# The down product of a feed forward as seven block products over four inner tiles, in turns with the up product

## The chip, the cores and the metric

The kernel runs on one core of one Trainium2 chip. The metric is the device time of one execution in microseconds (us), the median of several runs. A core has a matrix engine (TensorE, PE in the profile; its weight loads are PEld), three engines for elementwise work (VectorE or DVE, ScalarE or ACT, GpSimd or POOL) and a queue that issues transfers (SyncE, SP). SBUF is the on-chip memory, PSUM holds the sums of the matrix engine in eight banks, and HBM is the large memory outside.

## The reference

One layer of an encoder trunk for 2048 prompt tokens and 32 sample tokens, 1024 channels, all in float32. After a mixer (spatial gating and a gated delta rule, which the change does not touch) comes a feed forward with 4096 inner channels:

```python
h = rmsnorm(x, norm_ffn_g[l]) * (1 + sc2) + sh2
x = x + gt2 * (jnp.square(jax.nn.relu(h @ w_up[l])) @ w_down[l])
...
y = rmsnorm(x, final_norm_g)
```

`w_up` is 1024 x 4096 and `w_down` 4096 x 1024.

## The kernel before, in words

**Precision.** Every float32 operand of a matmul is kept as two parts in a reduced format: `hi` is a rounded copy (one ACT operation), `lo` the rest (one DVE subtraction, `split`). A product is three matmuls, hi·hi, hi·lo and lo·hi, into one PSUM bank (`mm3`); one matmul here is 128 x 128 weights against 260 token columns.

**Stages.** The mixer ends near 1047 us of the span; from there to the end runs the feed forward. Activations lie with channels on the partitions and tokens in the columns. The 2080 tokens are cut into four blocks `b` of 520, each of two column groups `g` of 260. The 4096 inner channels are cut into 16 pairs `s` of two 128-channel tiles `m`. For each block and each `s` the kernel computes the up product of that pair (`ffn_up`), squares its positive part, and adds its share to the down product (`ffn_down`, one step later), whose sums `acc` stay in SBUF for all 1024 outputs (eight tiles `m` by two groups `g`).

**Up product.** It is already done in a seven-product block form (in place of eight): the inputs of a block are combined once into seven sets of four tiles `hp[0..6]`, which go through HBM as `th_d` (`h2_values`, `h2_load`), and the weights of a pair are seven tiles of 128 x 512: three plain quadrants and four sums. In block 0 the sums are formed on POOL and stored to HBM (`su_d`); in later blocks they are read back as float32 and split again. Seven products of 12 matmuls are 84 matmuls for a pair.

**Down product.** Plain: for each `s`, each `g` and each of the eight outputs `m`, two inner tiles by three matmuls, 6 matmuls in a bank, then one DVE operation (`stt`, line 1574) which multiplies the bank by the gate and adds it to `acc`. For a pair that makes 96 matmuls and 16 DVE operations. The weights of a pair are two tiles of 128 x 1024, loaded and split (`down_weights`). The up product has four PSUM banks, the down product three. A hidden tile is relu and square on ACT, its square again on POOL in full precision, and the rest of it on DVE.

**End of a block.** The last pair squares the sums and adds them up, forms the norm of a token from them, scales, and writes `yT` (`final`); meanwhile the inputs of the next block are split into `hp`.

**Order.** The program is first recorded as operations with their regions of memory; a planner (`schedule`) then lays them out on the engines by readiness, by a class of urgency and, within the matmul classes, by the place of the matmul that they feed. It works with a table of costs that is written in the kernel, so the order on each engine is fixed before the run. All transfers are issued by SP, in one order, each waiting until its buffer is free. Buffers are taken in turn from rings.

## Time and profile before

| what | value |
|---|---|
| median of 3 runs | 2475.16 us (2473.93 to 2476.86) |
| profiled execution | 2478.63 us, span 2476.8 us |
| feed forward in it | 1047 to 2476.8 us |
| PE busy, of the span | 2422.7 us (98%) |
| DVE, ACT, POOL busy | 1870.6, 1256.6, 734.9 us |
| bytes moved | 461.00 MB, mean 186 GB/s |
| granted TensorE clock | 0.996 |

Busy time is the union of an engine's instructions. A matmul is shown with about 0.28 us, but they are pipelined, and one starts every 0.12 us; the same holds in a smaller measure on DVE and ACT, where an instruction starts before the one ahead has ended. So what an engine can do is read from the distance of starts, not from the durations. In the tables by stage the columns are the length of the stage, the busy time of each engine with its number of instructions, the granted clock (PEclk), the busy share of the 16 DMA engines and what they moved.

### The profile page before, as it was taken

To read this page: it belongs to the slowest core of one execution; us is meant where nothing else is said; L and a number is where in the kernel's file an instruction comes from. 1 tells how busy PE (TensorE), PEld (TensorE's weight loads), DVE (VectorE), ACT (ScalarE), POOL (GpSimd) and SP (SyncE) were. 2 spreads that over 40 slices of the span, in tenths; PEclk is the share of its full clock that TensorE was granted. 3 is DMA by queue.
4 is the path that set the end of the run, shared out by engine and by line. 5 is a ranking of instruction groups with operands and counts; after the bars stand their busy time and mean duration, and the time that the engine had idled before them with its cause. 6 is when DMAs were issued, how large, how long until landed. Compare 5 with 4: busy or idle time off the path is not lost.

```text
span 2476.8 us, 53101 instructions
## 1 busy us (share of the span) xinstructions
PE 2422.7 (98%) x19338; PEld 2271.0 (92%) x19338; DVE 1870.6 (76%) x4180; ACT 1256.6 (51%) x2840; POOL 734.9 (30%) x1072
## 2 busy tenths in 40 slices
PE   7999999999999999999999999999999999999998
PEld 3877788999989779999999999999999999999998
DVE  5556666556655555589988999888998888888887
ACT  4555556465565434454444654444754445644443
POOL 2134423212422223364443442111621111611112
PEclk9999999999999999999999999999999999999999
DMA  8688667455457767766554576444675444744431
GB/s 302 212 292 280 190 220 241 146 177 166 139 177 218 245 209 244 239 213 192 181 168 157 168 229 212 141 137 131 202 229 184 137 132 150 219 138 137 130 117 45
DMA packets 308750, 461.00 MB, mean 186 GB/s; under 512 B 62636, under 2 KB 192576, under 8 KB 308488
## 3 DMA queue, kind: packets, MB, share of 16 engines
q1 hardware_dynamic: 308488, 457.61, 58.7%
q8 instruction: 152, 2.49, 0.4%
q14 instruction: 110, 0.90, 0.1%
HBM read 354.59 MB, written 102.90 MB: 185 GB/s over the span
## 4 chain that ended last, share of the span: by engine, by line
PE 76%; DMA 8%; DVE 6%; ACT 3%; issue 3%; POOL 2%; SPq 1%; DVEq 0%; POOLq 0%; ACTq 0%
PE g L397 47%; PE u L397 21%; PE C L397 3%; DVE s L356 2%; POOL s L351 2%; PE B L397 2%; ACT s L336 2%; DVE s L351 2%; DVE wl L351 1%; PE L L397 1%; SPq L389 1%; PE M L397 1%; DMA s<-th_d 1%; ACT wh L336 1%; PE L L408 1%
## 5 line engine op out<-in xcount | busy, mean ns | idle before, releaser
L336 ACT ACTIVATE s<-s 128x260 f32<-128x260 f32 (+9 forms) x807 | 383.4, 481 | 615.1 <-PE g L397 430.9
L351 POOL TENSOR_TENSOR s<-s 128x260 f32<-128x260 f32 (+17 forms) x569 | 358.9, 634 | 897.4 <-ACT s L336 781.9
L356 DVE SCALAR_TENSOR_TENSOR s<-g,modc,s 128x260 f32<-128x260 f32 (+5 forms) x1200 | 526.1, 459 | 124.2 <-PE g L397 100.1
L397 PE MATMUL g<-s,s 128*128 128x260 f32 x4032 | 502.6, 284 | 5.9 <-DVE s L356 5.3
L397 PE MATMUL u<-BH,wh 128*128 128x260 f32 x1792 | 508.2, 284 | 0.0
L397 PE MATMUL u<-BL,wh 128*128 128x260 f32 x1792 | 506.4, 283 | 0.0
L397 PE MATMUL u<-BH,wl 128*128 128x260 f32 x1792 | 505.9, 282 | 0.4 <-DVE wl L351 0.4
L397 PEld LDWEIGHTS g<-s,s 128*128 128x128 f32 x4032 | 491.7, 188 | 10.4 <-DVE s L356 9.0
L397 PE MATMUL g<-BH,wh 128*128 128x512 f32 (+3 forms) x1144 | 431.7, 377 | 0.7 <-DVE s L356 0.7
L397 PE MATMUL g<-BH,wl 128*128 128x512 f32 (+3 forms) x1144 | 401.7, 351 | 0.0
L397 PE MATMUL g<-BL,wh 128*128 128x512 f32 (+3 forms) x1144 | 400.5, 350 | 0.8 <-DVE BL L351 0.8
L351 DVE TENSOR_TENSOR wl<-s,wh 128x512 fp32r<-128x512 f32 (+1 forms) x453 | 347.8, 781 | 28.2 <-ACT wh L336 24.1
L336 ACT ACTIVATE wh<-s 128x512 fp32r<-128x512 f32 (+1 forms) x453 | 284.8, 632 | 109.8 <-PE u L397 92.4
L397 PEld LDWEIGHTS u<-BH,wl 128*128 128x128 f32 x1792 | 337.2, 188 | 0.6 <-DVE wl L351 0.6
L397 PEld LDWEIGHTS u<-BH,wh 128*128 128x128 f32 x1792 | 337.5, 188 | 0.2
L397 PEld LDWEIGHTS u<-BL,wh 128*128 128x128 f32 x1792 | 337.5, 188 | 0.0
L351 POOL TENSOR_TENSOR s<-s,s 128x260 f32<-128x260 f32 (+3 forms) x195 | 222.4, 1150 | 296.2 <-ACT s L336 151.2
L351 DVE TENSOR_TENSOR s<-s,s 128x260 fp32r<-128x260 f32 (+7 forms) x400 | 237.7, 598 | 60.9 <-POOL s L351 30.8
L397 PE MATMUL g<-BH,s 128*128 128x260 f32 x1344 | 253.2, 285 | 4.3 <-DVE s L356 3.8
L397 PEld LDWEIGHTS g<-BH,wh 128*128 128x128 f32 x1144 | 217.1, 190 | 27.3 <-issue 9.1
L397 PEld LDWEIGHTS g<-BH,wl 128*128 128x128 f32 x1144 | 216.0, 189 | 19.4
L397 PEld LDWEIGHTS g<-BL,wh 128*128 128x128 f32 x1144 | 217.2, 190 | 15.4 <-DVE BL L351 1.5
(102 smaller groups left out, 3300.1 us busy)
## 6 DMA issues: line engine op xcount, KB each, us to landing
s<-w_u SPq DMA_DIRECT2D x208, 256.0 KB, 3.3
s<-su_d SPq DMA_DIRECT2D x192, 256.0 KB, 4.1
s<-w_d SPq DMA_DIRECT2D x64, 512.0 KB, 4.0
wr<-w_d SPq DMA_DIRECT2D x64, 512.0 KB, 5.2
wr<-w_b SPq DMA_DIRECT2D x42, 512.0 KB, 4.8
s<-x_d SPq DMA_DIRECT2D x128, 130.0 KB, 3.1
s<-adaw SPq DMA_DIRECT2D x32, 512.0 KB, 5.0
s<-kq_d SPq DMA_DIRECT2D x64, 256.0 KB, 3.3
```

What stands on the lines that cost most here:

```text
L336: self.p.op(ACT, c, lambda: nc.scalar.activation(out=R(out), in_=R(in_), func=func, **{k: R(v) for k, v in kw.items()}), [out, accum], [in ...
L351: self.p.op(eng, c, lambda: e.tensor_tensor(out=R(out), in0=R(a), in1=R(b), op=op), [out], [a, b])
L356: self.p.op(DVE, c, lambda: nc.vector.scalar_tensor_tensor(out=R(out), in0=R(a), scalar=R(s), in1=R(b), op0=op0, op1=op1), [out], [a, s, b])
L389: self.p.op(DMA, max(500, x), lambda: nc.sync.dma_start(out=R(out), in_=R(in_)), [out], [in_], lat=DMA_LATENCY + min(0, x - 500))
L397: nc.tensor.matmul(R(out), R(l), R(r), **kw)
L408: self.p.op(PE, 114, lambda: nc.tensor.transpose(R(out), R(in_), R(ident)), [out], [in_, ident])
```

## The change

**Down product.** Two pairs `s`, so four inner tiles, are taken together as `q` (eight per block). The four hidden blocks are B11 and B12 (first pair, groups 0 and 1) and B21, B22 (second pair). From them come T1 = B12 - B11, T2 = B22 - T1, T3 = B22 - B12 and T4 = B21 - T2 (`hidden`, on POOL), and each of the seven operands is split. The weights are combined the same way: three plain quadrants and four sums S1 to S4. Each half `u` of the outputs then takes seven products of 12 matmuls (`ffn_down`). A bank of the first set, B1, is filled by B11 and read, then T2 is added in the same bank and it is read again, and so on with T1 and B22: four reads of a bank that is never cleared between. Block 0, and the last `q` of the last block, stay plain with all four inner tiles in one bank (`ffn_down8`).

**Turns.** The up product of a pair is recorded behind each half `u` of the down product. All eight banks are one pool (`take`, `give`).

**Stored parts.** The four up sums of the weights are stored in block 0 as both parts, hi and lo (`su_d[s][i][e]`), and read back as two tiles with an ACT copy each, where one tile was read and split before. The sums of the down weights are stored in `sd_d`: for even `u` in block 0, for odd `u` in block 1.

**The rest.** The sums stay without gate until q = 6, when `settle` multiplies them by the gate and adds the residual; from then on `add` works with the gate. Every second lo part of the next block's inputs is formed on POOL. Half of the final scalings go from POOL and ACT to DVE. A hidden tile's lo part is taken from the ACT square.

```diff
-        self.su_d = [[dt(f"su_d{s}_{i}", [P, 512]) for i in range(4)] for s in range(16)]
+        self.su_d = [[[dt(f"su_d{s}_{i}{e}", [P, 512]) for e in range(2)] for i in range(4)] for s in range(16)]
+        self.sd_d = [[dt(f"sd_d{u}_{i}", [P, 512]) for i in range(4)] for u in range(16)]
...
-                self.split(*self.hp[i][k], x)
+                self.split(*self.hp[i][k], x, POOL if b and k % 2 else DVE)
...
+        def sum_(i, x):
+            if b == 0:
+                hl = self.operand(self.uw, x)
+                for e in range(2):
+                    self.dma(self.su_d[s][i][e], hl[e].f32())
+            else:
+                hl = self.turn(self.uw)
+                for e in range(2):
+                    self.act(hl[e], self.raw(self.uraw, self.su_d[s][i][e]), AF.Copy)
+            out.append(hl)
...
+        else:
+            for x in (quad(0), sd[2], sd[1], quad(1), sd[0], quad(3), sd[3]):
+                yield self.operand(self.dw, get(x))
+
+    def plain(self, b, q):
+        return b == 0 or (b, q) == (NB - 1, 7)
...
+                for u, _ in enumerate(self.ffn_down8(b, q, ops) if self.plain(b, q) else self.ffn_down(b, q, ops)):
+                    if q < 7 and u < 2:
+                        up(b, 2 * q + 2 + u, then)
...
-                for so, sw, q in self.fsegs(b, g):
-                    ss = slice(so, so + sw)
-                    self.stt(a[:, ss], ps[:, ss], self.modc[:, 5, m, q : q + 1], x[:, ss] if s == 0 else a[:, ss], ALU.mult, ALU.add)
...
+        if q == 0 and first:
+            self.act(a, ps, AF.Copy)
+        elif q < SETTLE:
+            self.tt(a, ps, a, ALU.add)
...
+            product("T3", B2, True, w[u])
+            add(B2, hi, 1, True)
+            product("T2", B1[u], False, w[u])
+            add(B1[u], hi, 0, True)
+            B3 = [self.take() for _ in lo]
+            product("B21", B3, True, w[u])
+            add(B3, lo, 0, last=True)
+            self.give(*B3)
+            product("T1", B1[u], False, w[u])
+            add(B1[u], hi, 1, last=True)
+            product("T4", B2, False, w[u])
+            add(B2, hi, 0, last=True)
+            self.give(*B2)
+            product("B22", B1[u], False, w[u])
+            add(B1[u], lo, 1, True, True)
+            self.give(*B1[u])
+            yield
```

**How it moves the order on DVE.** In the middle of a block, the additions of the down product. `g` and `f` are PSUM banks, a number is one use of a bank, `s_289` to `s_292` (before) and `s_417` to `s_420` (now) are pieces of SBUF that hold the sums, `modc` the gate. Before:

```order
L356 SCALAR_TENSOR_TENSOR s_289<-g_23630,modc,s_289 128x260
L356 SCALAR_TENSOR_TENSOR s_289<-g_23638,modc,s_289 128x260
L356 SCALAR_TENSOR_TENSOR s_290<-g_23646,modc,s_290 128x260
L356 SCALAR_TENSOR_TENSOR s_290<-g_23654,modc,s_290 128x260
L356 SCALAR_TENSOR_TENSOR s_291<-g_23662,modc,s_291 128x260
L356 SCALAR_TENSOR_TENSOR s_291<-g_23670,modc,s_291 128x260
```

Now:

```order
L352 TENSOR_TENSOR s_418<-f_18467,s_418 128x260
L352 TENSOR_TENSOR s_418<-f_18478,s_418 128x260
L352 TENSOR_TENSOR wl<-wr_96,wh 128x512
L352 TENSOR_TENSOR s_420<-f_18483,s_420 128x260
L352 TENSOR_TENSOR s_420<-f_18487,s_420 128x260
L352 TENSOR_TENSOR s_9896<-s_426,s_10062 128x512
L352 TENSOR_TENSOR s_420<-f_18467,s_420 128x260
L352 TENSOR_TENSOR s_10863<-s_428,s_10863 128x260
L352 TENSOR_TENSOR s_420<-f_18478,s_420 128x260
```

A bank was read once and left; now the banks `f_18467` and `f_18478` are read, filled further, and read again, with splits of weights (128x512) and of hidden tiles (`s_10863`) between.

**How it moves the order on PE.** At the same place, with `f_18467` and `f_18478` the two banks of B1. Before, one output of the down product, in one bank:

```order
L397 MATMUL g_19415<-BH_78,s_925 128x260
L397 MATMUL g_19415<-BL_86,s_925 128x260
L397 MATMUL g_19415<-BH_78,s_9976 128x260
L397 MATMUL g_19415<-BH_78,s_10697 128x260
L397 MATMUL g_19415<-BL_86,s_10697 128x260
L397 MATMUL g_19415<-BH_78,s_9859 128x260
```

Now, the third product, T2, into the banks that B11 had filled 12 matmuls of T3 before:

```order
L398 MATMUL f_18487<-BH_78,s_10105 128x260
L398 MATMUL f_18467<-s_10865,s_1053 128x260
L398 MATMUL f_18467<-s_11827,s_1053 128x260
L398 MATMUL f_18467<-s_10865,s_10105 128x260
L398 MATMUL f_18467<-BH_78,s_1053 128x260
L398 MATMUL f_18467<-BL_86,s_1053 128x260
L398 MATMUL f_18467<-BH_78,s_10105 128x260
L398 MATMUL f_18478<-s_10865,s_1053 128x260
```

An output takes as many matmuls in one visit to a bank as before, but the bank has to have been read before the visit begins.

**How it moves the order on SP.** In the middle of a block, reads of weights. Before:

```order
L389 DMA s_277<-su_d_1_214 128x512
L389 DMA s_298<-w_d 128x1024
L389 DMA wr_96<-w_d 128x1024
L389 DMA s_278<-su_d_0_213 128x512
L389 DMA s_278<-su_d_2_215 128x512
L389 DMA s_279<-w_u 128x512
```

Now:

```order
L390 DMA s_406<-su_d_10_263 128x512
L390 DMA s_412<-x_d_195 128x260 x2
L390 DMA s_406<-su_d_11_264 128x512
L390 DMA s_426<-sd_d_0_357 128x512
L390 DMA wr_96<-su_d_00_261 128x512
L390 DMA wr_96<-su_d_01_262 128x512
L390 DMA s_406<-w_u 128x512
L390 DMA s_426<-su_d_21_266 128x512
```

A sum of the up weights is now two transfers (`su_d_10`, `su_d_11`), and the down weights come as plain quadrants and sums (`sd_d`) of 128 x 512.

More of the change, by code (lines that the diff above doesn't have):

```diff
@@ L33 @@
 NB = T // (2 * G)
+SETTLE = 6
 SLABW = 8 * WZ
@@ L1433, in up_weights @@
+        plain = lambda q, x: out.append(self.operand(self.uw, x if b == 0 else self.raw(self.uraw, quad(q))))
+        if b:
+            s1 = s2 = s3 = s4 = a11 = a12 = a22 = None
+        plain(0, a11)
+        sum_(1, s2)
+        sum_(0, s1)
+        if b == 0:
+            s3 = self.turn(self.uraw) if len(self.uraw) > 6 else a11
             self.tt(s3, a11, a21, ALU.subtract, POOL)
+        sum_(2, s3)
+        if b == 0:
+            s4 = s2
             self.tt(s4, a12, s2, ALU.subtract, POOL)
-            for i, x in enumerate((s1, s2, s3, s4)):
-                self.dma(self.su_d[s][i], x)
@@ L1510, in ffn_up, with up @@
-    def ffn_up(self, b, w):
-        rs = self.rt.pop(0)
-        self.rt.append(rs)
-        W, Z, X, Y = (self.bank("u")[:, :G] for _ in range(4))
-        def product(i, ps, start):
+        def up(b, s, ops):
+            self.ffn_up(b, s, self.up_weights(b, s), ops)
+            if (b, s) == (0, 15):
+                self.uraw = self.draw = self.draw + self.uraw[:4]
+                self.era(2, F32R)
+            if s == 8 and b < NB - 1:
+                self.h2_values(b + 1)
+            if s == 15 and b < NB - 1:
+                self.h2_load(b + 1)
@@ L1517, in product, with take, give, ffn_up @@
+    def take(self):
+        b = self.fbanks.pop(0)
+        self.banks["f"] = [b]
+        return b, self.bank("f")[:, :G]
+    def give(self, *banks):
+        self.fbanks += [b for b, _ in banks]
+    def ffn_up(self, b, s, w, ops):
+        e = s % 2
+        def product(n, i, ps, start):
             for k in range(4):
-                n = slice(128 * k, 128 * k + 128)
+                c = slice(128 * k, 128 * k + 128)
                 with self.p.at(GEMM):
-                    self.mm3(ps, w[i][0][:, n], w[i][1][:, n], *self.hp[i][k], start and k == 0, k == 3, skip_group_check=True)
+                    self.mm3(ps[1], w[n][0][:, c], w[n][1][:, c], *self.hp[i][k], start and k == 0, k == 3, skip_group_check=True)
+        def place(m, g):
+            if self.plain(b, s // 2):
+                return self.new("fk")
+            return self.new("fr") if e else self.keep[g][m]
@@ L1522, in finish @@
         def finish(m, g, t, src=None):
-            rh, rl = rs[m][g]
             self.act(t, t if src is None else src, AF.Relu)
-            self.act(rh, t, AF.Square)
-            q = self.new("fq")
-            self.tt(q, t, t, ALU.mult, POOL)
-            self.tt(rl, q, rh.f32(), ALU.subtract)
-        product(0, W, True)
+            self.act(t, t, AF.Square)
+            self.hidden(b, s, m, g, t, ops)
+        if s == 0:
+            self.keep = [[self.new("fk") for _ in range(2)] for _ in range(2)]
@@ new lines, in ffn_up, with hidden, put @@
+        self.give(Y)
+    def hidden(self, b, s, m, g, t, ops):
+        def put(name, x):
+            ring = self.rp8 if b == 0 else self.rpb if s % 2 else self.rpa
+            ops.setdefault(name, {})[m] = self.operand(ring, x)
+        if self.plain(b, s // 2):
+            return put((s % 2, g), t)
+        k0, k1 = self.keep[0][m], self.keep[1][m]
+        if s % 2 == 0 and g == 0:
+            put("B11", t)
+            self.tt(k0, k1, t, ALU.subtract, POOL)
+            put("T1", k0)
+        elif s % 2 and g == 1:
+            self.tt(k1, t, k1, ALU.subtract, POOL)
+            put("T3", k1)
+            self.tt(k0, t, k0, ALU.subtract, POOL)
+            put("T2", k0)
+            put("B22", t)
+        elif s % 2:
+            put("B21", t)
+            self.tt(t, t, k0, ALU.subtract, POOL)
+            put("T4", t)
@@ L1572, in ffn_down, with settle @@
+    def settle(self, b):
+        for m in range(KT):
+            for g in range(2):
+                a, x = self.acc[m][g], self.new("fe")
+                t0 = 2 * G * b + G * g
+                self.dma(x, self.x2_d[m][:, t0 : t0 + G])
                 for so, sw, q in self.fsegs(b, g):
                     ss = slice(so, so + sw)
[L1574 to L1583 removed]
@@ new lines, in square @@
+    def square(self, b, m, g):
+        end = (b, g) == (NB - 1, 1)
+        a = self.acc[m][g]
+        if self.ssq[g] is None or self.ssq[g][0] != b:
+            sa = self.new("fs")
+            self.ssq[g] = [b, sa]
+            self.act(sa, a, AF.Square)
+            return
+        x = self.new("fp" if end and m == 7 else "fx")
+        self.act(x, a, AF.Square)
+        sa = self.ssq[g][1]
+        if end and m in (6, 7):
+            self.ssq[g].append(x)
+        else:
+            self.tt(sa, sa, x, ALU.add, DVE if end else POOL)
```

298 lines of the change are left out of this document (172 added, 126 removed).

## The prediction

> **What bounds the kernel now.** The page's busy times come first, then the table by stage.
>
> ```profile
> PE 2422.7 (98%) x19338; PEld 2271.0 (92%) x19338; DVE 1870.6 (76%) x4180; ACT 1256.6 (51%) x2840; POOL 734.9 (30%) x1072
> ...
> PEclk9999999999999999999999999999999999999999
> ```
> ```profile
> core 0: us, PE busy (x) PEld busy (x) DVE busy (x) ACT busy (x) POOL busy (x), PEclk, DMA share, GB/s
> 1047.00:1400.00 353.00, 348.27 (x2855) 343.94 (x2855) 318.27 (x597) 173.46 (x352) 149.34 (x137) 1.00 0.57 180
> 1400.00:1745.00 345.00, 343.38 (x2836) 341.41 (x2835) 300.42 (x584) 174.77 (x353) 88.38 (x104) 1.00 0.54 170
> 1745.00:2092.00 347.00, 344.74 (x2847) 342.67 (x2846) 301.08 (x585) 179.91 (x367) 89.62 (x106) 1.00 0.56 172
> 2092.00:2440.00 348.00, 346.04 (x2861) 344.23 (x2860) 305.06 (x668) 164.14 (x325) 80.87 (x96) 1.00 0.45 141
> 2440.00:2476.80 36.80, 27.31 (x223) 26.19 (x221) 25.27 (x71) 10.96 (x27) 13.47 (x19) 0.90 0.18 59
> ```
> The four middle rows are the four token blocks: TensorE idles 4.7, 1.6, 2.3 and 2.0 us in them, at full clock. A busy TensorE could still be a slow one, so the chain of waits is read next.
>
> ```profile
> 1614.74 10.07 PE u L397 x84
> 1624.81 11.65 PE g L397 x96
> 1636.46 10.07 PE u L397 x84
> ```
> Up product (u), down product (g), with nothing between. A matmul starts every 10.07/84 = 0.1199 us in the one, 11.65/96 = 0.1213 us in the other. A block is 16 x (84 + 96) = 2880 matmuls, 16 x 21.72 = 347.5 us: the length of the stages. TensorE's count of matmuls sets the end. What it waits for otherwise (waits from 1400 to 2440 us; total, times, longest) is little:
>
> ```profile
> PEld g L397 <- DVE s L356: 7.8, 11, 1.8
> PE g L397 <- DVE s L356: 5.6, 7, 1.6
> ```
>
> **The matmuls removed.** In a pair of pairs (a q) the down product has 192 matmuls; seven block products make 2 halves x 7 x 12 = 168. The seven-product form holds in blocks 1 and 2 (eight q each) and seven q of block 3, so 23 x 24 = 552 matmuls go, at 0.1213 us: -67.0 us (-66.2 at the up product's distance). The order on TensorE shows the same number. A q then needs 168 x 0.1199 + 168 x 0.1213 = 40.5 us in place of 43.4; everything else has to fit into that.
>
> **DVE and ACT per q.** Starts, not durations, count. Timeline rows of DVE and ACT (start, length from first start to last end):
>
> ```profile
> 1606.71 1.31 DVE L356 SCALAR_TENSOR_TENSOR s<-g,modc,s 128x260 f32<-128x260 f32 x3
> ...
> 1704.63 0.43 DVE L351 TENSOR_TENSOR s<-u,s 128x260 f32<-128x260 f32 x1
> 1704.98 1.28 DVE L351 TENSOR_TENSOR wl<-s,wh 128x512 fp32r<-128x512 f32 x2
> ...
> 1776.73 2.39 DVE L351 TENSOR_TENSOR wl<-s,wh 128x512 fp32r<-128x512 f32 x2
> ```
> ```profile
> 1603.14 0.62 ACT L336 ACTIVATE wh<-s 128x512 fp32r<-128x512 f32 x1
> 1603.66 0.86 ACT L336 ACTIVATE s<-s 128x260 f32<-128x260 f32 x2
> ...
> 1750.13 0.40 ACT L336 ACTIVATE BH<-s 128x260 fp32r<-128x260 f32 x1
> 1750.44 0.40 ACT L336 ACTIVATE s<-s 128x260 f32<-128x260 f32 x1
> ```
> On DVE a 260-wide addition takes 0.35 us of the queue (1704.63 to 1704.98), a gated one (1.31 - 0.49)/2 = 0.41, a 512-wide split 1.28 - 0.68 = 0.60. On ACT the 512-wide copy takes 0.52, a 260-wide operation 0.31.
>
> DVE in a q from block 1 on: the 14 splits of up weights become 6 (three plain tiles, two pairs), since four stored sums need none; the four 1024-wide splits of down weights become 14 of 512; 10 additions of the up product stay; hidden-tile splits go from 8 to 14; 32 gated additions become 28 plain ones. Sum: 20 x 0.60 + (10 + 14 + 28) x 0.35 = 30.2 of 40.5 us. The trace's 300.42/8 = 37.6 busy us per q, in which overlapping durations are joined, is no measure for this sum; by durations,
>
> ```profile
> L356 DVE SCALAR_TENSOR_TENSOR s<-g,modc,s 128x260 f32<-128x260 f32 x634 | 298.6, 484 | 64.4 <-PE g L397 61.6 <-DMA yT<-s 2.2
> L351 DVE TENSOR_TENSOR wl<-s,wh 128x512 fp32r<-128x512 f32 x330 | 243.2, 749 | 15.3 <-ACT wh L336 11.9
> L351 DVE TENSOR_TENSOR s<-u,s 128x260 f32<-128x260 f32 x239 | 101.0, 423 | 17.5 <-PE u L397 13.8 <-ACT s L336 2.9 <-issue 0.3
> L351 DVE TENSOR_TENSOR s<-s,s 128x260 fp32r<-128x260 f32 x128 | 66.7, 523 | 10.8 <-POOL s L351 10.5
> ```
> (groups from 1400 to 2440 us) it is 20 x 0.749 + 38 x 0.423 + 14 x 0.523 = 38.4 us, still under 40.5. I take DVE as covered.
>
> ACT: 14 copies of up weights become 3 plain + 8 stored parts per pair, 22; 14 copies for down weights; p1, relu and square stay 18; hidden copies go from 8 to 14: 36 x 0.52 + 32 x 0.31 = 28.6 of 40.5 us, from a busy 174.77/8 = 21.8. It rises most, and fits. POOL takes 8 subtractions per q where 8 squares went; at the 1.01 us of the row below, 8.1 us. So in the middle of a block: nothing.
>
> ```profile
> L351 POOL TENSOR_TENSOR s<-s,s 128x260 f32<-128x260 f32 x60 | 59.4, 1009 | 46.3 <-DMA s<-x_d 46.3
> ```
>
> **Transfers.** A q now loads 22 + 14 = 36 tiles of 256 KB (0.262 MB), 9.4 MB in 40.5 us, 233 GB/s, where it loaded 14 x 0.262 + 4 x 0.524 = 5.8 MB. What a block moves beside weights is 1400 to 1745's 345 x 170 GB/s = 58.7 MB less 8 x 5.8, so about 12.5 MB, and blocks 1 and 2 need 88 MB in 324 us, 272 GB/s. What the engines can give (transfers from 1425 to 1475 us; and a stage of the mixer):
>
> ```profile
> DMA packets 8719, 12.19 MB, mean 244 GB/s; under 512 B 969, under 2 KB 5733, under 8 KB 8712
> ...
> q1 hardware_dynamic: 8712, 12.11, 77.8%
> ...
> s<-su_d SPq DMA_DIRECT2D x12, 256.0 KB, 4.0
> ```
> ```profile
> 124.00:186.00 62.00, 61.60 (x303) 44.55 (x303) 34.15 (x74) 35.55 (x56) 20.36 (x24) 1.00 0.87 293
> ```
> 244 GB/s at a share of 0.778 makes an estimated 313 GB/s at full share, and TensorE stayed fed at 293. So the mean fits at a share near 0.87. The eight raw buffers of a q's 36 tiles turn over every 40.5 x 8/36 = 9.0 us; landing 4.0, ACT 0.52 and DVE 0.60 leave over 3 us for queues on SP and the engines.
>
> **Two places where it doesn't fit smoothly.** First the change of blocks. The stages there before:
>
> ```profile
> 1395.00:1420.00 25.00, 25.00 (x208) 24.58 (x207) 22.08 (x46) 18.69 (x44) 20.56 (x24) 1.00 0.59 178
> 1420.00:1445.00 25.00, 24.27 (x198) 23.65 (x197) 24.17 (x39) 16.34 (x36) 19.53 (x20) 1.00 0.83 253
> ...
> 2090.00:2115.00 25.00, 24.90 (x202) 24.32 (x201) 24.22 (x60) 15.69 (x36) 9.78 (x12) 1.00 0.54 163
> 2115.00:2140.00 25.00, 25.00 (x205) 24.38 (x204) 22.34 (x36) 19.68 (x46) 24.38 (x25) 1.00 0.68 209
> ```
> TensorE lost up to 0.7 us. Now the last q (20.4 us) and two up products (20.1) have to cover 36 weight tiles, 28 input tiles and 16 output tiles of 0.133 MB: 9.4 + 5.9 = 15.3 MB, at 313 GB/s 48.9 us against 40.5. So each of three changes costs between 0 (part is loaded ahead, or written later) and 8.4 us. I take 4, half: +12. SP issues all of it in one order, so late output tiles keep weights behind them waiting, and those hold ACT, DVE and then TensorE. Second, h2_values from q = 3 on adds 44 tiles of 0.133 MB, 5.9 MB, to a q's 9.4: 48.9 us in one q, but nobody needs these before the block's end. 0, at most 3 x 8.4 = 25.
>
> **Block 0** keeps its 2880 matmuls. POOL forms four 512-wide sums a q more, for the down weights, and eight squares less; DVE has 16 additions in place of 32. Its idle TensorE, 353 - 347.5 = 5.5 us, bounds the gain; the loss I bound by as much again. 0 taken. The end of the program is the same chain of squares, norm, scaling and output: 0.
>
> **Sum.** -67.0 + 12 = -55 against the profiled 2478.63: 2423.6. The runs' median, 2475.16, lies 3.5 below that execution: **2420 us**. With all of the small terms at their good end 2405 (-67 - 5.5, rounded up a little); with changes of block, h2_values and block 0 at their bad end -67 + 25 + 25 + 5.5 = -11, 2464, which supposes all of them at once. The forecast's own range is 2405 to 2437.
>
> **The rivals.**
> *Transfers take over; slower (7%).* For it: by the order on SP there are 192 more reads and 64 more writes of up sums, 152 reads and 64 writes of down sums, and 218 reads of 256 KB for 128 of 512 KB: (192 + 64 + 152 + 64 + 218 - 256) x 0.262 = 113.8 MB more than now's 461 (page), all issued in one order, and no stretch of the feed forward shown above ran over 253 GB/s. Against it: 293 held for 62 us. If 244 GB/s were all that lasts, blocks 1 and 2 would take 88/0.244 = 361 us, 15 longer each; block 0 (63.5 MB now, 25 more for stored sums) 363, 10 longer; block 3 (49 + 28 MB) would stay with TensorE, 20 shorter: +20, 2495. It decides from 3 x 88/(353 + 345 + 347 + 20) = 248 GB/s downward. The Trainium skill, "DMA: Bandwidth & Descriptors", section "Bandwidth", speaks for this rival: it asks for transfers of 1 MiB or more and has 138 GB/s for one of 64 KB, 341 for 1 MB; no run here shows one transfer alone, and the 293 GB/s row, with many in flight, does not bear it out.
>
> *The bank is not read in time; no gain (6%).* In each half of the outputs four products begin in a bank that DVE must have read: 184 waits over 23 q. At the mean wait shown, 7.8/11 = 0.7 us, half of them waiting would cost 65 us: 2475 - 67 + 65 = 2473. Against it: 12 matmuls, 1.45 us, lie between, while DVE needs two additions, 0.7 us; the rest is for its queue and the signals.
>
> *DVE is held up by POOL (4%).* The row of 2.39 us for two splits, while POOL worked without a break, is 1.2 us a split. All 20 splits at that and 14 hidden ones at 0.55 would make 20 x 1.2 + 7.7 + 13.3 = 45 us a q, 4.5 over: +104, slower, 2512. Against it: POOL works about 8 of 40 us.
>
> *Changes of block and h2_values cost their upper ends; faster by less (19%).* 2437 to 2464.
>
> **How the numbers follow.** Forecast 64%, and the four rivals as given. A median of this kernel tells 0.2%, 5 us, from no change. Faster: 64 + 19 and half of the second rival, 86%; same 3%; slower 11%. The range runs from 2405 to 2456 and leaves out the slower rivals, the one without gain and a small part of the last.
>
> **What would show it.** In the profile after: 552 matmuls fewer and a start every 0.12 us; stages of about 325 us for blocks 1 and 2 and 328 for block 3, block 0 near 350; DVE and ACT busy near nine tenths and eight tenths; DMA share near 0.85 there. If TensorE's idle time sits at the changes of block behind DMA, the 12 us were the right term; if it is spread over all q behind DVE at banks, the second rival; if the landing of weights rises well over 4 us all through, the first. A block 1 over 345 us would prove the forecast wrong.

## The result and the profile after

The changed kernel takes **2434.54 us** (median of 4 runs, 2432.48 to 2436.47), the kernel before in the same session 2476.01 us (4 runs, 2473.93 to 2480.10). The ratio is **0.983, 95% interval 0.9813 to 0.9847**: 41.5 us less, where 55 had been forecast. The profiled execution took 2435.92 us with a span of 2434.1.

From the page of the changed kernel: busy times, transfers and the time from issue to landing of a weight tile (last column, us).

```profile
PE 2360.2 (97%) x18786; PEld 2202.6 (90%) x18786; DVE 1754.4 (72%) x4041; ACT 1563.6 (64%) x3729; POOL 782.3 (32%) x1079
...
DMA packets 389688, 574.85 MB, mean 236 GB/s; under 512 B 71629, under 2 KB 201569, under 8 KB 389417
...
s<-su_d SPq DMA_DIRECT2D x288, 256.0 KB, 4.0
s<-w_u SPq DMA_DIRECT2D x168, 256.0 KB, 4.2
```

The matmuls went from 19338 to 18786, exactly 552 fewer. The bytes rose by 574.85 - 461.00 = 113.85 MB, the 113.8 MB of the prediction. A weight tile lands in 4.0 to 4.2 us; before, a stored sum took 4.1 and a plain tile of `w_u` 3.3. The counts are right, then, and the difference must lie in waiting. The table by stage of the changed kernel, cut at the changes of block (about 1399, 1735 and 2081 us, by the count of matmuls):

```profile
core 0: us, PE busy (x) PEld busy (x) DVE busy (x) ACT busy (x) POOL busy (x), PEclk, DMA share, GB/s
1047.00:1400.00 353.00, 348.09 (x2877) 345.54 (x2876) 269.42 (x490) 203.74 (x467) 154.02 (x123) 1.00 0.75 252
1400.00:1677.00 277.00, 273.43 (x2246) 269.99 (x2246) 238.36 (x501) 227.57 (x513) 105.18 (x105) 1.00 0.82 269
1677.00:1812.00 135.00, 124.83 (x984) 120.25 (x983) 113.13 (x222) 108.31 (x261) 66.80 (x71) 0.99 0.79 254
1812.00:2037.00 225.00, 222.66 (x1843) 221.28 (x1841) 192.65 (x435) 177.40 (x396) 39.87 (x50) 1.00 0.82 266
2037.00:2172.00 135.00, 126.20 (x1008) 121.72 (x1007) 110.03 (x226) 111.53 (x271) 55.34 (x64) 1.00 0.78 254
2172.00:2380.00 208.00, 206.75 (x1712) 205.59 (x1711) 170.28 (x394) 156.29 (x349) 32.72 (x40) 1.00 0.73 237
```

Stretches of the same length around the same changes in the kernel before:

```profile
1692.00:1827.00 135.00, 132.75 (x1087) 130.93 (x1086) 119.93 (x237) 79.96 (x174) 54.86 (x60) 1.00 0.63 190
...
2060.00:2195.00 135.00, 132.98 (x1090) 131.23 (x1089) 121.82 (x259) 77.98 (x169) 52.78 (x58) 1.00 0.58 180
```

The number in brackets behind PE says more than the busy time, since a delayed matmul can still be counted as busy. 135 us hold 1125 matmuls at 0.12 us. Before, 1087 and 1090 began there; now 984 and 1008. So each of these two changes of block loses about 17 and 14 us, against 4 to 5 before. In the middle of block 1 (1400 to 1677), 2246 matmuls are 269.5 us of 277.

Taken over the whole feed forward in stretches of 45 us, from 1047 to 2397 us, 45 minus 0.12 us per matmul gives a loss of 45.6 us after and 17.8 before, 28 more. Some 22 of this lie at the two changes, 6 in the middles of blocks 1 and 2, 2 in block 3, and block 0 is 3 better. Minus 66 for the matmuls, plus 28, and minus 3 because the feed forward began at 1043.9 instead of 1047.1 us, makes -41; the two profiled executions differ by 42.7. (That start varies from profile to profile, over all kernels shown here from 1038.3 to 1047.7 us.) Seen by blocks, and by the count of matmuls, the four take 355, 336, 346 and 343 us, where they took 357, 353, 354 and 353.

### What happens at a change of block

The changed kernel around the change from block 1 to block 2 (first four rows), from 2 to 3, and, for comparison, from block 0 to 1, where the last `q` is plain:

```profile
1690.00:1710.00 20.00, 20.00 (x169) 20.00 (x168) 19.17 (x40) 15.74 (x37) 6.83 (x7) 1.00 0.92 302
1710.00:1730.00 20.00, 18.18 (x146) 17.37 (x144) 18.51 (x37) 15.62 (x39) 18.27 (x20) 1.00 0.55 166
1730.00:1750.00 20.00, 16.24 (x117) 14.53 (x118) 14.00 (x28) 15.90 (x37) 12.84 (x15) 1.00 0.94 312
1750.00:1770.00 20.00, 17.04 (x123) 15.95 (x122) 14.30 (x27) 16.74 (x46) 13.66 (x18) 0.91 0.68 211
2050.00:2070.00 20.00, 19.23 (x153) 18.26 (x151) 16.13 (x36) 15.16 (x43) 14.29 (x17) 1.00 0.51 157
2070.00:2090.00 20.00, 18.56 (x148) 17.84 (x148) 17.93 (x36) 15.83 (x36) 11.29 (x14) 1.00 0.88 288
...
1380.00:1400.00 20.00, 20.00 (x170) 20.00 (x169) 15.57 (x30) 15.82 (x41) 16.02 (x20) 1.00 0.91 293
```

The prediction expected transfers at their limit here. The opposite comes first: from 1710 to 1730 the DMA engines fall to a share of 0.55, while DVE (18.51 of 20 us) and POOL (18.27) are full. Then everything comes at once, 0.94 at 312 GB/s, and TensorE loses most. What SP waited for between 1690 and 1770 (us in all, times, longest):

```profile
SPq L390 <- DVE BL L352: 11.3, 10, 3.7
SPq L390 <- DVE s L352: 8.3, 13, 1.7
SPq L390 <- POOL BL L352: 7.1, 11, 1.4
...
SPq L390 <- POOL s L352: 5.4, 3, 2.6
```

`BL` is the lo part of the next block's inputs. SP cannot issue the next input tile until the subtraction that frees its buffer is done, and all weights behind it in SP's order wait too. The last row is three stores (`sd_d`) of the sums of down weights that POOL forms in block 1 for odd `u`; SP stands until each sum is ready. At the change from block 2 to 3 no such sums are formed. The subtractions themselves, in the same stretch (min/median/max in ns):

```profile
L352 DVE TENSOR_TENSOR BL<-s,BH x22: 415/434/1508, 1709.2 to 1771.6; 128x260 fp32r<-128x260 f32 x22
L352 POOL TENSOR_TENSOR BL<-s,BH x14: 754/1180/1329, 1704.0 to 1733.4; 128x260 fp32r<-128x260 f32 x14
```

A lo part on POOL takes 1.18 us at the median, where its fastest took 0.754, and one on DVE up to 1.51 us. The last `q`'s subtractions T1 to T4, and here the four sums of down weights, want POOL in the same 20 us; its 28 additions, splits of weights and hidden tiles want DVE.

### The profile page after: what moved, and what is told of

The parts are those of the page before. It is cut to its first block, busy times and chain, and to the rows that moved or that the text cites. A ratio compares the mean times of both kernels' runs of the same rounds, so it can differ in the third digit from the quotient of the medians.

```text
span 2434.1 us, 53576 instructions
## 1 busy us (share of the span) xinstructions
PE 2360.2 (97%) x18786; PEld 2202.6 (90%) x18786; DVE 1754.4 (72%) x4041; ACT 1563.6 (64%) x3729; POOL 782.3 (32%) x1079
## 2 busy tenths in 40 slices
DMA packets 389688, 574.85 MB, mean 236 GB/s; under 512 B 71629, under 2 KB 201569, under 8 KB 389417
## 4 chain that ended last, share of the span: by engine, by line
PE 60%; DMA 14%; DVE 10%; ACT 8%; issue 5%; POOL 3%; SPq 1%; POOLq 0%; DVEq 0%; ACTq 0%
PE f L398 30%; PE g L398 21%; DVE s L352 5%; ACT s L337 4%; PE C L398 3%; POOL s L352 2%; DMA s<-su_d 2%; DVE s L357 2%; PE B L398 2%; ACT wh L337 2%; DVE wl L352 2%; PE L L398 1%; DMA s<-w_u 1%; PE M L398 1%; DMA s<-x_d 1%
## 5 line engine op out<-in xcount | busy, mean ns | idle before, releaser
L398 PE MATMUL f<-s,s 128*128 128x260 f32 x3984 | 537.2, 283 | 7.2 <-DVE s L352 3.8
L398 PE MATMUL f<-BH,wh 128*128 128x260 f32 x1800 | 513.3, 285 | 12.4 <-DVE s L352 9.2
L398 PE MATMUL f<-BH,wl 128*128 128x260 f32 x1800 | 510.3, 284 | 4.7 <-DVE wl L352 4.1
L398 PEld LDWEIGHTS f<-s,s 128*128 128x128 f32 x3984 | 500.2, 188 | 12.5 <-DVE s L352 6.2
L398 PE MATMUL f<-BL,wh 128*128 128x260 f32 x1800 | 508.5, 283 | 1.3 <-DVE BL L352 1.1
L352 DVE TENSOR_TENSOR s<-s,s 128x512 fp32r<-128x512 f32 (+5 forms) x740 | 418.5, 582 | 76.7 <-ACT s L337 42.8
L398 PE MATMUL g<-BH,wh 128*128 128x512 f32 (+2 forms) x1112 | 421.5, 379 | 0.0
L352 DVE TENSOR_TENSOR s<-f,s 128x260 f32<-128x260 f32 x856 | 346.0, 422 | 95.1 <-PE f L398 91.5
L398 PE MATMUL g<-BH,wl 128*128 128x512 f32 (+2 forms) x1112 | 391.9, 352 | 0.0
L398 PE MATMUL g<-BL,wh 128*128 128x512 f32 (+2 forms) x1112 | 390.8, 351 | 0.6 <-DVE BL L352 0.6
L398 PEld LDWEIGHTS f<-BH,wh 128*128 128x128 f32 x1800 | 339.3, 188 | 16.8 <-DVE s L352 6.4
L357 DVE SCALAR_TENSOR_TENSOR s<-s,s,s 128x512 f32<-128x512 f32 (+6 forms) x318 | 165.2, 536 | 73.0 <-ACT s L337 41.8
```

The costliest lines, as they stand in the source:

```text
L352: self.p.op(eng, c, lambda: e.tensor_tensor(out=R(out), in0=R(a), in1=R(b), op=op), [out], [a, b])
L357: self.p.op(DVE, c, lambda: nc.vector.scalar_tensor_tensor(out=R(out), in0=R(a), scalar=R(s), in1=R(b), op0=op0, op1=op1), [out], [a, s, b])
L398: nc.tensor.matmul(R(out), R(l), R(r), **kw)
```

## The experiments

Ratios are to the kernel before in the same session (for the experiments its median was between 2477.96 and 2480.33), so they compare across sessions better than the times. The loss comes from one profiled execution of each kernel, and executions of one kernel differ by 4 to 14 us, so a few us of loss tell little; the first kernel with a plain last `q` was profiled in its fastest execution, 2411.14 us. And the planner lays out the whole program anew for each kernel, so an edit at one place also moves the order elsewhere. The loss is 45 us minus 0.12 us per matmul, summed over stretches of 45 us: at the two changes 1677 to 1812 and 2037 to 2172, and over the middles 1407 to 1677 and 1812 to 2037 together. A stretch without any wait reads about -0.3 by this measure, since matmuls that cross its edges count on both sides.

| kernel | median, us | ratio, 95% interval | loss at change 1 to 2 | at change 2 to 3 | middles |
|---|---|---|---|---|---|
| the change | 2434.54 | 0.9830 (0.9813 to 0.9847) | 16.4 | 13.4 | 8.6 |
| last `q` plain | 2420.17 | 0.9759 (0.9736 to 0.9782) | 3.0 | 1.1 | 7.7 |
| stored up sum read once | 2422.67 | 0.9774 (0.9759 to 0.9788) | 16.8 | 10.2 | 1.6 |
| up sums stored in float32 | 2457.68 | 0.9918 (0.9900 to 0.9935) | 42.2 | 11.4 | 6.5 |
| inputs split on DVE alone | 2436.50 | 0.9831 (0.9813 to 0.9849) | 12.4 | 9.4 | 15.2 |
| gate from q = 2 | 2436.46 | 0.9839 (0.9821 to 0.9856) | 22.2 | 13.0 | 7.0 |
| down product plain everywhere | 2457.63 | 0.9921 (0.9901 to 0.9940) | 1.3 | -0.4 | -1.6 |
| last `q` plain, halves as in block 0 | 2422.51 | 0.9774 (0.9754 to 0.9794) | 4.0 | 3.7 | 8.4 |
| the same, float32 sums mid-block | 2430.74 | 0.9810 (0.9786 to 0.9834) | 23.5 | 3.2 | 6.1 |
| inputs without lo parts | 2429.37 | 0.9786 (0.9756 to 0.9816) | 8.5 | 10.6 | 9.2 |
| fewer additions in the last `q` | 2435.67 | 0.9817 (0.9803 to 0.9832) | 13.8 | 12.5 | 11.6 |
| float32 mid-block, gate from q = 2 | 2438.01 | 0.9827 (0.9813 to 0.9842) | 26.3 | 8.6 | 4.6 |
| float32 mid-block, next inputs urgent | 2434.22 | 0.9815 (0.9798 to 0.9831) | 7.2 | 1.9 | 17.5 |

### The last q plain: is the loss at the changes the last q's work?

```diff
-        return b == 0 or (b, q) == (NB - 1, 7)
+        return b == 0 or q == 7
```

> The last q of every block is plain (it is seven products in blocks 1 and 2 of the change): 48 matmuls more, +5.8 us, and at the two changes of block 6 weight tiles, 12 additions and 8 POOL subtractions fewer. In the changed kernel TensorE loses 16 us around 1677 to 1812 and 13 us around 2037 to 2172, against none at the change from block 0 to 1, whose last q is plain. Theory A (transfers: at these changes more is to be moved than the DMA engines carry in the time) and theory B (engine work: DVE is full there, 10.0 of 10 us busy) both expect the loss to fall to some 2 us each: 2434.5 + 5.8 - 25 = 2415. If the time rises by 6 us instead, the loss has nothing to do with the form of the last q.

In this kernel two of the eight weight tiles of the second half of the last `q` take the place of ones of the first half (there are six weight buffers in blocks 1 and 2) before both groups have used them, so part of the output of these blocks is something else; the amount of work and the order of the loads are those of a plain last `q`.

Measured 2420.17 us. The loss at the changes went from 16.4 and 13.4 us to 3.0 and 1.1, though 48 matmuls (5.8 us) came back. The loss sits in the seven-product form of the last `q` beside the inputs of the next block. The middles still lose 7.7.

With the two halves in the order of block 0 as well, nothing is replaced too early and the whole computation is kept:

```diff
-        for g, u in ((0, 0), (0, 1), (1, 0), (1, 1)) if b else ((0, 0), (1, 0), (0, 1), (1, 1)):
+        for g, u in ((0, 0), (0, 1), (1, 0), (1, 1)) if (b, q) == (NB - 1, 7) else ((0, 0), (1, 0), (0, 1), (1, 1)):
```

> The last q of blocks 1 and 2 plain, as in e1_plain_last, but with the two halves of the outputs one after the other as in block 0, so that the six weight buffers hold. Matmuls +5.8 us. Theory B (DVE bounds the change of block when the last q is in seven products): the loss from 1677 to 1812 and from 2037 to 2127 falls from 28 to some 5 us, 2434.5 + 5.8 - 23 = 2417. If the order of the halves in e1_plain_last was what helped: 2430 or more.

2422.51 us: **this version beats both kernels**, and its interval (0.9754 to 0.9794) lies below that of the change (0.9813 to 0.9847). Its change from block 1 to 2:

```profile
1710.00:1730.00 20.00, 19.90 (x164) 19.43 (x163) 16.88 (x34) 18.23 (x48) 10.09 (x12) 1.00 0.95 307
1730.00:1750.00 20.00, 18.90 (x157) 18.48 (x156) 12.47 (x25) 13.08 (x31) 15.61 (x20) 1.00 0.70 214
```
```profile
L352 DVE TENSOR_TENSOR BL<-s,BH x22: 416/430/975, 1713.0 to 1770.8; 128x260 fp32r<-128x260 f32 x22
L352 POOL TENSOR_TENSOR BL<-s,BH x14: 737/760/1093, 1708.2 to 1739.1; 128x260 fp32r<-128x260 f32 x14
```

With a plain last `q`, POOL is busy 10.09 us of these 20 instead of 18.27, a lo part on it takes 0.76 us instead of 1.18, the DMA share is 0.95 instead of 0.55, and the 28 input tiles are issued within 57 us (1676.5 to 1733.7) instead of 81 (1671.7 to 1752.8). From 1690 to 1770 us SP waits 5.7 us for lo parts instead of 18.4. What the plain form leaves out is not T1 to T4 alone: 6 weight tiles, 12 additions and 6 hidden splits go as well, and at this change the four sums of down weights on POOL with the stores for which SP stood. No run takes these apart from T1 to T4. The Trainium skill, "SBUF — State Buffer", section "Who interferes with whom", has a DVE instruction with two SBUF inputs contend with a GpSimd instruction that reads SBUF. The two medians agree with this, though no run here sets the two engines side by side alone.

### Which work of the last q?

Three kernels each move or leave out one part of what meets there: POOL's share of the input splits, 12 of the 28 additions of the last `q`, and the lo parts altogether.

```diff
-                self.split(*self.hp[i][k], x, POOL if b and k % 2 else DVE)
+                self.split(*self.hp[i][k], x)
```

> Only the move of every second lo part of the next block's inputs to POOL is undone: 14 splits of 0.35 us, 4.9 us, go back to DVE at each change of block from block 1 on, and as much as 14 us of POOL go. Theory A: no difference, within 2 us. Theory B: 3 to 10 us longer; if POOL's holding up DVE is what fills DVE there, shorter by as much.

2436.50 us, no difference from the change in the whole (0.9831 and 0.9830), but the parts differ: the two changes lose 8 us less (12.4 and 9.4), the middles 6.6 more, where the order is another one too. At the change POOL is now relieved and DVE is full, and the DMA share stays low:

```profile
1710.00:1730.00 20.00, 18.44 (x147) 17.58 (x146) 19.56 (x40) 16.72 (x43) 9.71 (x9) 1.00 0.64 209
```

```diff
         a = self.acc[m][g]
+        if b in (1, 2) and q == 7 and not first:
+            return
```

> In the last q of blocks 1 and 2, 12 of the 28 gated additions are left out (those of B21, T1 and T4), 4.9 us of DVE at each of the two changes, and with them the waits of the products that go into the same banks; their sums are missing in the result. The squares stay. If the additions of the last q are the cause: loss at the changes down by 6 to 10 us each, 2434.5 - 16 = 2418. If the chain of inputs is: 2430 to 2434.

2435.67 us, ratio 0.9817 with an interval that overlaps that of the change. The additions of B21, T1 and T4 are missing in the sums, and nothing else changes in the amount of work.

```diff
-                self.split(*self.hp[i][k], x, POOL if b and k % 2 else DVE)
+                if b:
+                    self.act(self.hp[i][k][0], x, AF.Copy)
+                else:
+                    self.split(*self.hp[i][k], x)
```

> From block 1 on the inputs of a block get only their hi part (28 copies on ACT); the 14 subtractions on DVE (0.35 us each, 4.9 us) and the 14 on POOL for the lo part are left out, and the lo parts of block 0 are used on. Transfers and matmuls stay. If what TensorE waits for at the change is the chain of inputs (transfer, copy, subtraction, buffer free, next transfer) or POOL's share in it, the loss there (16 and 12 us) falls by more than half: 2434.5 - 16 = 2418. If it is the additions and splits of the last q on DVE: 4.9 us of DVE less help a little, 2428 to 2432.

2429.37 us, ratio 0.9786; blocks 1 to 3 work with the lo parts of block 0. At the change from block 1 to 2 the loss fell from 16.4 to 8.5 us; at the next hardly (13.4 to 10.6). The row of 1710 to 1730 in the kernel with fewer additions:

```profile
1710.00:1730.00 20.00, 18.21 (x137) 17.80 (x136) 16.13 (x28) 14.71 (x39) 17.72 (x19) 0.91 0.44 137
```

And in the kernel without lo parts:

```profile
1710.00:1730.00 20.00, 19.55 (x159) 19.01 (x158) 16.97 (x37) 19.30 (x54) 11.48 (x12) 1.00 0.84 262
```

In these two rows the DMA share follows POOL (17.72 us with 0.44, 11.48 with 0.84), not DVE (16.13 and 16.97). But with the inputs split on DVE alone POOL was as free (9.71) and the share 0.64, with DVE at 19.56, so POOL alone does not set it. At the two changes together the kernel with POOL's lo parts moved to DVE loses 8 us less than the change, the one without any lo parts 11 less, and a plain last `q` 22 to 26 less. So the lo parts of the inputs likely hold some 8 to 11 us of the loss; leaving out 12 of the 28 additions changed it by 3.5, less than executions differ. The time without lo parts, 2429.37, is even the one that was expected if DVE's own work were the cause (2428 to 2432); the additions left out speak against that. What makes up the rest, T1 to T4, the sums of down weights with their stores, the other additions or the weight tiles, stays open.

### The gate earlier

```diff
-SETTLE = 6
+SETTLE = 2
```

> Only the place of settle moves, from q = 6 to q = 2: 16 gated additions (0.41 us each, 6.6 us of DVE) and 16 transfers of 0.133 MB leave the stretch ahead of the change of block; in return the additions of q = 2 to 5 carry the gate, 28 x 0.06 = 1.7 us more DVE in each of these q. If DVE bounds the change of block, the loss there falls by up to 6 us at each of two changes, 2434.5 - 10 = 2424; if transfers do, by 2.1 MB / 313 GB/s = 6.7 us at most as well, but then DVE's busy share there would stay as it is. If settle lies too early to matter for the change: 2434 within 3.

2436.46 us, the last of the three expectations; the loss at the first change even rose to 22.2. Moving the 16 tiles that `settle` loads does not relieve the change.

### The middle of a block: reads or DVE?

```diff
+                x = self.raw(self.uraw, self.su_d[s][i][0])
                 for e in range(2):
-                    self.act(hl[e], self.raw(self.uraw, self.su_d[s][i][e]), AF.Copy)
+                    self.act(hl[e], x, AF.Copy)
```

> Of a stored sum of the up weights only the hi part is read from block 1 on, and both copies are made from it (the lo part of these weights is wrong by that): 192 transfers of 256 KB, 50 MB, fewer; the work of TensorE, ACT, DVE and POOL is the same. Theory A: the loss at the two changes falls from 16 and 13 us to under 5 each, 2434.5 - 20 = 2414. Theory B: as the changed kernel, within 4 us.

2422.67 us, between the two expectations. The gain is not where theory A had it: the two changes still lose 27 us, the middles 1.6 instead of 8.6.

```diff
-                hl = self.operand(self.uw, x)
-                for e in range(2):
-                    self.dma(self.su_d[s][i][e], hl[e].f32())
+                self.dma(self.su_d[s][i][0], x)
             else:
-                hl = self.turn(self.uw)
-                for e in range(2):
-                    self.act(hl[e], self.raw(self.uraw, self.su_d[s][i][e]), AF.Copy)
+                x = self.raw(self.uraw, self.su_d[s][i][0])
+            hl = self.operand(self.uw, x)
```

> Only the stored parts are undone: a sum of the up weights is stored in float32 once, read as one tile and split again. 67 MB fewer moved; per q 8 splits of 0.60 us more on DVE (30.2 to 35 of 40.5 us), 8 copies fewer on ACT than with two parts. Theory A: the loss at the changes falls, in the middle nothing happens: 2420 to 2426. Theory B: DVE is what is short, so the loss at the changes grows by the 4.8 us of DVE in every q there: 2440 to 2450.

2457.68 us, beyond even what theory B had: **the stored parts are worth 23 us** against this form. The same stretch, 1452 to 1677 us, in the change:

```profile
1452.00:1677.00 225.00, 221.50 (x1819) 218.76 (x1819) 197.09 (x423) 178.96 (x394) 75.37 (x75) 1.00 0.82 270
```

with one read of each stored sum:

```profile
1452.00:1677.00 225.00, 224.12 (x1858) 222.88 (x1857) 200.24 (x431) 177.25 (x395) 76.13 (x74) 1.00 0.69 217
```

and with the sums in float32:

```profile
1452.00:1677.00 225.00, 221.35 (x1839) 220.53 (x1838) 217.85 (x444) 151.90 (x342) 73.70 (x72) 1.00 0.63 196
```

At a DMA share of 0.69, with DVE and ACT as busy as in the change, 1858 matmuls begin instead of 1819: 39 x 0.12 = 4.7 us. So the second reads cost the middle of block 1 its few us; the changes (16.8 and 10.2 us) hardly moved. Whether it is the transfers themselves, at a share of 0.82, or the second raw tile that each stored sum takes, this edit does not tell, since it takes away both. How it reaches TensorE is not shown either. In the change, from 1400 to 1677 us, TensorE's matmuls wait 3.3 us, all for DVE, for an addition that reads a bank or the lo part of a hidden tile:

```profile
PE f L398 <- DVE s L352: 1.9, 4, 1.1
PE f L398 <- DVE BL L352: 1.4, 4, 0.4
```

One weight load waits longer (1.3 us, at 1562.6), for a copy that itself waits 1.1 us for a sum of down weights from POOL. With float32 sums DVE is busy 217.85 of 225 us. Until 1632 us TensorE loses nothing by that, and then 42.2 us at one change. What TensorE waited for there (1677 to 1722 us), and the chain that ended last, in pieces:

```profile
PE f L398 <- DVE s L357: 12.1, 2, 11.5
```
```profile
1684.43 6.02 DMA s<-x_d
1690.45 0.07 issue
1690.52 0.73 POOL s L352
...
1695.30 2.21 DMA s<-x_d
1697.52 0.02 issue
1697.54 0.50 DVE s L357
```

The 11.5 us are `settle` (L357): its tiles from `x_d` come from the ring that `h2_values` of the next block uses as well. With DVE full, that work, which nobody needs before the end of the block, is put off (its last store leaves at 1698.9 us, in the change at 1631.6), and then holds what the block needs now. The prediction gave h2_values 0 because nobody waits for them; they hold buffers all the same. That this is the cause, the two kernels below that move one or the other bear out: the wait at this place goes in both.

### Can the two gains be had together?

From here on the last `q` is plain, and the sums of the pairs 2 to 13 are stored in float32, so that DVE is relieved at the ends of a block and the transfers in its middle:

```diff
+                if 2 <= s < 14:
+                    self.dma(self.su_d[s][i][0], x)
...
+            elif 2 <= s < 14:
+                hl = self.operand(self.uw, self.raw(self.uraw, self.su_d[s][i][0]))
```

> e7_plain_last, and the up sums of the pairs s = 2 to 13 are stored once in float32 and split again, as in e3_f32_sums, those near the change of block (s = 0, 1, 14, 15) keep both parts. In the middle of a block 8 transfers of 256 KB fewer per q and 8 DVE splits more. My theory has two causes: transfers in the middle (loss of some 12 us there in the changed kernel, none in e3_f32_sums), DVE at the changes. Then this loses in neither place: e7_plain_last less 8 to 10 us. If DVE is what is short everywhere, it is slower than e7_plain_last by 5 to 20 us.

2430.74 us: not the gain of the theory, but the loss of its alternative (5 to 20 us slower than with a plain last `q` alone). The middle is nearly clean up to 1632 us (1.2), but 25 us are lost between 1632 and 1722 in the same way: 9.4 us in one wait for `settle`. Two attempts to move this wait. With the gate from q = 2 (as above):

> e8_plain_mix with settle at q = 2. In e8_plain_mix and in e3_f32_sums TensorE lost some 20 us once, near 1690 us, in a wait of 9.4 or 11.5 us for the gated additions of settle, whose residual tiles come through the same six buffers as the tiles from which the inputs of the next block are formed, and these were late. With settle ahead of those the one loss goes; the rest of e8_plain_mix lost little: 2430.7 - 20 + 4 (28 x 0.06 us of gate in four q of three blocks, hidden at best) = 2411 to 2415, below every kernel so far. If the loss comes back at the change of block instead, 2425 or more.

2438.01 us, the worse of the two expectations: the loss moved into the change itself, 20.9 us from 1722 to 1767, where TensorE waited for inputs:

```profile
PE f L398 <- ACT BH L337: 9.8, 2, 6.8
```

Here the last store of h2_values leaves at 1739.0 us, after the loads of the next inputs have begun. With h2_values in a more urgent class:

```diff
-                self.h2_values(b + 1)
+                with self.p.at(LOCAL):
+                    self.h2_values(b + 1)
```

> e8_plain_mix with the forming of the next block's inputs (h2_values) in a more urgent class of the planner, so that it is done where it is recorded, at q = 3, and not in what DVE has left. In e8_plain_mix and e3_f32_sums the last of its 28 stores was issued at 1693.6 and 1698.9 us, in the changed kernel and e7_plain_last at 1631.6 and 1635.5; the 20 us lost near 1690 fell there. If the late inputs are the cause, that loss goes, some 4 us per block may be lost at q = 3 instead where DVE is taken away: 2430.7 - 20 + 8 = 2419 or less, as e7_plain_last or below. If DVE is simply too full with the sums split again, the loss moves to another place and the time stays at 2428 or more.

2434.22 us, the worse expectation again. The stores now leave from 1465.5 to 1511.8 us for the next block, the wait for `settle` is gone, and the changes lose 7.2 and 1.9. But 11 us are lost from 1452 to 1542, where this work now stands ahead of the weights, and 6.7 at the start of block 2's middle. In all three places where they were put with float32 sums, the 44 tiles cost time.

### The rest of the change without the seven products

The down product plain in all blocks, no sums of its weights formed or stored; turns, shared banks, stored parts, late gate and the rest stay:

```diff
-        return b == 0 or (b, q) == (NB - 1, 7)
+        return True
...
-            if b == 0 and u % 2 == 0:
+            if False:
```

> The change without its core: the down product is plain in every block (four inner tiles in a bank, no sums of down weights formed, stored or read), while turns, stored up parts, settle and the shared banks stay. 552 matmuls more than the changed kernel. By the matmul term alone it takes 66 to 67 us more; by my theory the losses of TensorE that came with the change (27 us more than before it) nearly all hang on the seven-product form, so 2434.5 + 66.5 - 22 = 2479. If the rest of the change had its own cost or gain, it shows here against the kernel before.

2457.63 us, a miss of 21 us on the good side: **without the seven products, the rest still takes about 20 us off**. This kernel is not the change less its core in every respect. The plain form with four inner tiles in a bank, which the change has in block 0 and in one `q` of block 3, now stands everywhere, with 16 additions a `q` where the change has 28 and the kernel before 32; the halves come in the order of block 0, and the hidden tiles have block 0's ring of 16 operands. Its page, two pieces of its chain of waits, and its stretches at the changes:

```profile
PE 2410.1 (98%) x19338; PEld 2265.6 (92%) x19338; DVE 1492.9 (61%) x3485; ACT 1433.9 (58%) x3453; POOL 526.3 (21%) x831
```
```profile
1466.06 281.05 PE f L398 x2342
...
2110.73 326.05 PE f L398 x2718
```
```profile
1677.00:1812.00 135.00, 133.63 (x1108) 132.64 (x1107) 82.93 (x168) 102.55 (x251) 36.57 (x44) 1.00 0.76 238
2037.00:2172.00 135.00, 135.00 (x1123) 134.34 (x1122) 78.44 (x157) 99.38 (x240) 33.90 (x40) 1.00 0.70 221
```

The matmuls are as many as before (19338), but they run without a break for 281 and 326 us, at 281.05/2342 = 0.1200 us. Before, the down product ran at 0.1213. That is not a slower matmul. Take the starts of the down product's matmuls from 1400 to 2380 us: where two follow within 0.16 us, they lie 0.1201 us apart before, 0.1196 in this kernel and 0.1197 in the change. But 73 starts came later than that before, by 0.1 us each in the mean, and 20 here. Such late starts, most of them too short for the tables of waits, make most of the difference. By the measure of the table, TensorE's loss from 1047 to 2397 us falls from 17.8 to 1.2 us: 5 in block 0, whose stretch 1047 to 1400 us starts 2897 matmuls instead of 2855, 7 at the changes, which lose 1.3 and -0.4 us instead of 3.6 and 3.8, and 5 in the rest. The last 3 of the 20 us lie outside this stretch, 2 of them in the start of the feed forward (1044.8 us).

## Why the prediction was right and wrong

**The forecast that held.** Faster, by the count of matmuls: 552 fewer, about 66 us, to the matmul. 2434.5 lies in the range, near the upper end of the likeliest case's own (2405 to 2437). The stages do not come out as said: blocks 1, 2 and 3 take 336, 346 and 343 us, forecast were 325, 325 and 328. Part of this is that a block took 353 us before, by its matmuls, and not 347.5: the rows read as blocks hold 2836 to 2861 matmuls, and a block has 2880. DVE and ACT fit as said: in the middle of block 1 (the row 1452 to 1677 of the change) DVE is busy 197.09/225 = 0.88, ACT 0.80, the DMA share 0.82, close to the nine tenths, eight tenths and 0.85 of the prediction.

**Changes of block, "I take 4, half: +12".** This term failed, in size and in mechanism. The change from block 0 to 1 costs nothing (170 matmuls start in the 20 us from 1380), the other two cost 13 and 10 us over what they lost before, 22 in all, above the 8.4 that the term allowed for one. It was sized by bytes over the speed of the DMA engines. But the DMA share falls to 0.55 and 0.51 there: SP's one order stands behind work of DVE and POOL, at the first change longest (18.4 us) behind input tiles whose buffers these two have not freed. The prediction had the right sentence on SP's order, with the wrong holder: late output tiles in place of the input tiles. It counted the DMA issues of the change, and not that DVE and POOL must work off 28 input tiles in the same 20 us as T1 to T4 and the last additions; the 8.1 us of POOL per `q` were called covered by a mean over the `q`. For block 1 that sum also leaves out the four sums of down weights that POOL forms there for each odd `u`: from 1400 to 1677 us POOL is busy 105.18 us, in the middle of block 2, 39.87 of 225. That the seven-product form of the last `q` causes this loss is shown by leaving it out; which of its parts does is not: without the lo parts beside it the loss is 8 to 11 us smaller, the others were not taken apart.

**"So in the middle of a block: nothing."** Mis-sized by 6 us in blocks 1 and 2 and 2 in block 3. With 50 MB fewer reads the loss of the middles falls from 8.6 to 1.6 us. So the reads, or the buffers that they take, matter at a mean share of 0.82 too; by which wait they reach TensorE is open.

**"Block 0 ... 0 taken", "The rest."** The prediction gave the new order, the shared banks and the fewer DVE operations no gain in TensorE. By the plain kernel, which has four inner tiles to a bank everywhere, they bring about 20 us. Against it the seven products bring only (0.9921 - 0.9830) x 2476 = 23 us of their 66; 43 go to the waits that they bring with them (a loss of 45.6 us against 1.2). Two errors partly cancelled: that the total is nearer than its terms is partly luck.

**The rivals.** *Transfers take over* (2495): no; most weight tiles land in 4.0 to 4.3 us, and 302 and 312 GB/s were reached for 20 us. Its weaker form, reads as the cause in the middle, holds for some 7 us, with the reservation above. *The bank is not read in time* (2473): no. Leaving out 24 additions at the changes moved nothing that can be told, and TensorE's largest group of waits in the changed kernel, 1400 to 2380 us, has 15 waits where this rival needed some 90, and 12 of them, 6.9 us, are for an addition that reads a bank:

```profile
PE f L398 <- DVE s L352: 9.4, 15, 1.4
```

*DVE held up by POOL* (2512): not as a state of all `q`, but around the change (1690 to 1780 us) a lo part on POOL takes 1.18 us at the median and one on DVE up to 1.51. *Changes of block and h2_values at their upper ends* (2437 to 2464): the result lies just below it, by the changes alone; what h2_values cost in the change itself no run shows (the whole middle of block 1, where they are formed, loses 6 us); they cost some 25 us as soon as DVE is full (float32 sums).

## What to carry to other kernels

When matmuls are taken from a kernel bound by TensorE, the gain is kept in the steady part and given back where phases meet: list for that stretch, and not for a mean, what each engine must do before a buffer comes free. Here a queue that issues in one order turned a full elementwise engine into idle transfers, so where the DMA share is low beside waiting weights, look for who holds a buffer, or keeps a store waiting, ahead of them. The plain form in one of eight steps cost 5.8 us of matmuls and still made the kernel 12 us faster. And undo the core of a change alone: what remains of it may have a gain of its own that hides the price of the core.

## What the runs showed of the hardware

The clock that TensorE is granted can fall after a wait of less than 2 us, and the stall then costs more than its wait. The kernel with a plain last `q` and float32 sums mid-block, 1670 to 1700 us, and some of its matmuls in and after the first waits (in brackets the wait and what ended it):

```profile
1670.00:1680.00 10.00, 4.25 (x20) 3.23 (x18) 7.90 (x12) 8.48 (x18) 5.73 (x7) 0.68 0.85 266
1680.00:1690.00 10.00, 2.53 (x11) 2.23 (x10) 4.17 (x9) 3.35 (x6) 2.25 (x3) 0.50 0.79 244
1690.00:1700.00 10.00, 5.49 (x30) 5.23 (x30) 5.39 (x13) 1.23 (x2) 0.00 (x0) 0.63 0.82 248
```
```profile
1672.42 0.39 PE L398 MATMUL f<-BH,wh 128*128 128x260 f32 x1 [1.73 <-ACT wh L337]
...
1673.67 0.42 PE L398 MATMUL f<-BH,wl 128*128 128x260 f32 x1
1673.89 0.42 PE L398 MATMUL f<-BH,wh 128*128 128x260 f32 x1
1674.11 0.42 PE L398 MATMUL f<-BL,wh 128*128 128x260 f32 x1
```

The granted clock is 0.50 from 1680 to 1690 us. Matmuls start 0.22 us apart in place of 0.12 from 1673.67 us on, 1.3 us after a wait of 1.73 us. From 1632 to 1722 us the waits of TensorE's matmuls make 19.2 us, and 25 are lost. The Trainium skill, "TensorE: Matmul & The Clock Gate", section "What's actually happening", gives half the clock after an idle window of about 3.4 us; the trace agrees on the half, but here a wait of half that length was enough. In the first kernel with a plain last `q` a single wait of 1.30 us, at 1729.7 us, comes ahead of a row of 20 us with a granted clock of 0.91.

The other unexpected number, 0.1213 us a matmul of the down product before and 0.1200 in the plain kernel, is not a distance that depends on how many matmuls visit a bank: visits of six run at 0.1197 us in the change, where no start is late. The difference is mostly late single starts; what makes those late, no run shows.
